# First stage of a hybrid decoder step: norm and scale in one VectorE instruction, the shift inside the rounding, scale and shift halves summed and turned separately

## The chip, the cores and the metric

The kernel runs on one core of one Trainium2 chip. The metric is device time in microseconds (us) of one execution, as the median of several runs. Engines are named TensorE (PE in the rows; PEld is its weight load), VectorE (DVE), ScalarE (ACT), GpSimd (POOL) and SyncE (SP, which issues most of the loads). Matmuls collect in PSUM; everything else lives in SBUF.

## The reference, cut to what matters

One inference step of a one-layer decoder on 512 prompt tokens and 8 sample tokens, width 1024. The first stage computes

```
mod = silu(c) @ w_mod + b_mod                 # shift, scale, gate, ... ; one row for the prompt, eight for the samples
h   = rmsnorm(x, norm1_g) * (1 + scale1) + shift1
u   = h @ w_in                                # first three column tiles of 128: f, q and output gate of head 0
```

The recurrences, the gates, the output projection and the MLP follow and are not touched by the change.

## The kernel before, in words

The tokens stand in the free dimension: activations are held turned, as 8 blocks k = 0..7 of 128 features by 520 tokens (512 of the prompt, 8 samples). Each matmul operand is split in a high half, rounded to the fast matmul format (`h_hi`, `whi`), and a low half, what the rounding lost (`h_lo`, `wlo`). A product (j, k) is six matmuls: weight tile j, block k, as high x high, high x low, low x high, for two halves of the tokens.

The first stage is written in `begin`. `load_x` asks for x; `norm_x` squares it on ScalarE and takes the root on VectorE with thirteen tiny operations (`rsqrt_small`); `transposed` turns all eight blocks of x on TensorE and copies them out of PSUM into `self.x`, half on ScalarE and half on VectorE; `normed` turns the roots into a row that lies on every partition (`rsb`). `scaled` multiplies a block by `rsb` into `u`. A **session** (k, part) is the product of silu(c) with 256 columns of `w_mod`, for blocks k and k + 1; part 1 is the scale, part 0 the shift. Both parts of a block pair go into the two halves of one PSUM tile. One ScalarE copy (`modev`) brings them out, and **turn** (`mod_close`) turns the four 128x128 squares and lets VectorE sum them and add the bias, into `modT`. Then `affine_split` makes the halves of two blocks: ScalarE computes the high half with scale and shift as it rounds, VectorE computes the same in full (`ht`) and subtracts. `high(j)` on ScalarE and `low(j)` on VectorE split weight tile j the same way; the third weight tile, `third` (tile `w` in the rows), is loaded last of the three.

The order on each engine is that of the code: `order("p", ...)`, `order("a", ...)` and `order("v", ...)` tie every instruction of TensorE, ScalarE and VectorE behind the one before it in program text. An engine works its queue strictly in that order, so an instruction that waits holds all behind it. SyncE's loads go out in the order in which `begin` asks for them. GpSimd issues the small parameter loads.

The three products j = 0, 1, 2 of the eight blocks are mixed with the sessions, so that TensorE has work while the next pair's scale and shift are made. `products((0, 2), ...)` are the first that need block pair 2, 3. In ScalarE's queue the high halves of that pair stand behind `high(2)`.

## Time and profile before

| what | value |
|---|---|
| median of 3 runs | 1004.61 us (1003.96 to 1005.44) |
| the profiled execution | 1004.8 us, its span from first to last instruction 1003.0 us |
| TensorE busy | 981.2 us, 98% of the span |
| VectorE, ScalarE, GpSimd busy | 694.2, 513.4, 112.4 us |
| TensorE idle until its first matmul | 3.11 us |

The first stage fills about the first 50 us. A busy share is a mean over all stages; what an edit is worth there is read from the waits of that stage. Line numbers Lnnn are those of the kernel before. In the rows "mm<-h,whi 128x260 x4" is four matmuls into tile `mm` from the tiles `h` and `whi`; what stands in brackets behind a row is how long the engine sat idle before it, and what ended that.

### The profile page before, as it was taken

How to read it: one execution, taken by the hardware profiler on the slowest of the kernel's cores; microseconds unless marked ns; L12 is line 12 of the kernel's file. 1: busy time of each engine (PE TensorE's matmuls, PEld its weight loads, DVE VectorE, ACT ScalarE, POOL GpSimd, SP SyncE). 2: the span in 40 equal slices, each digit the busy share in tenths (PEclk: the TensorE clock that was granted, in tenths of full speed). 3: DMA queues.
4: the chain of work that ended last, by engine and by line, in shares of the span. 5: the costliest groups of instructions: out<-in, count | busy, mean ns of one | idle time of the engine just before them, and what ended most of it. 6: DMA issues, size and time to landing. Idle time of an engine off the chain costs nothing.

```text
span 1003.0 us, 23261 instructions
## 1 busy us (share of the span) xinstructions
PE 981.2 (98%) x9585; PEld 954.5 (95%) x9585; DVE 694.2 (69%) x1546; ACT 513.4 (51%) x987; POOL 112.4 (11%) x194
## 2 busy tenths in 40 slices
PE   6999999999999999999999999999999999999996
PEld 4799999999999999999989999999999999999996
DVE  6789698697878867563332347767766776777686
ACT  5444844664584456351222234466556645646664
POOL 3000000000000000120000000012321331232151
PEclk9999999999999999999999999999999999999998
DMA  9885435344434434686567765222762483274242
GB/s 299 239 257 146 133 102 155 95 146 137 117 105 133 127 98 126 208 272 193 167 190 228 231 183 157 85 85 53 168 160 71 102 194 99 54 174 91 63 85 86
DMA packets 212572, 145.78 MB, mean 145 GB/s; under 512 B 6262, under 2 KB 196878, under 8 KB 212458
## 3 DMA queue, kind: packets, MB, share of 16 engines
q1 hardware_dynamic: 202562, 132.37, 44.5%
q0 software_dynamic: 9904, 11.92, 6.4%
q8 instruction: 75, 1.23, 0.5%
q14 instruction: 31, 0.25, 0.1%
HBM read 123.61 MB, written 13.39 MB: 137 GB/s over the span
## 4 chain that ended last, share of the span: by engine, by line
PE 93%; ACT 2%; SPq 2%; DVE 1%; DMA 1%; issue 1%; DVEq 0%; ACTq 0%
PE mm L120 67%; PE ps L1152 8%; PE pt L1152 4%; PE pb L1152 2%; PE ps L629 2%; PE ps L385 1%; PE pb L780 1%; DMA w<-in_w_in_dram 1%; SPq L374 1%; PE pt L705 1%; SPq L74 1%; PE pt L718 1%; PE pt L629 1%; PE pt L720 1%; PE ps L395 0%
## 5 line engine op out<-in xcount | busy, mean ns | idle before, releaser
L120 PE MATMUL mm<-h,whi 128*128 128x260 f32 x3040 | 502.8, 285 | 2.9 <-ACT h L481 1.9
L120 PEld LDWEIGHTS mm<-h,whi 128*128 128x128 f32 x3040 | 421.5, 189 | 8.4 <-ACT h L481 2.6
L120 PE MATMUL mm<-h,wlo 128*128 128x260 f32 x1520 | 310.8, 284 | 0.0
L85 ACT CAST whi<-wst 128x1024 fp32r<-128x1024 f32 x165 | 172.6, 1048 | 217.6 <-PE mm L120 178.7
L88 DVE TENSOR_TENSOR wlo<-wst,whi 128x1024 fp32r<-128x1024 f32 x165 | 201.2, 1220 | 89.6 <-ACT whi L85 88.2
L120 PEld LDWEIGHTS mm<-h,wlo 128*128 128x128 f32 x1520 | 237.0, 189 | 0.0
L120 PE MATMUL mm<-a,whi 128*128 128x260 f32 x512 | 82.8, 283 | 0.0
L120 PEld LDWEIGHTS mm<-a,whi 128*128 128x128 f32 x512 | 70.3, 188 | 0.9 <-issue 0.8
L120 PE MATMUL mm<-a,wlo 128*128 128x260 f32 x256 | 51.7, 284 | 0.0
L881 POOL DMA_DIRECT2D t<-oaT_d x8 | 4.3, 549 | 383.9 <-DMA oaT_d<-e 377.1
L1248 DVE TENSOR_TENSOR f<-f 128x260 f32<-128x260 f32 x64 | 27.3, 427 | 28.9 <-ACT f L1243 28.2
L1240 POOL TENSOR_TENSOR ft<-ft,fsh 128x8 f32<-128x8 f32 x28 | 18.4, 658 | 215.8 <-DVE ft L1234 215.8
L1237 ACT ACTIVATE ft<-ft,fsh 128x512 f32<-128x512 f32 (+2 forms) x36 | 24.1, 676 | 36.0 <-DVE ft L1234 36.0
L120 PE MATMUL mm<-b,whi 128*128 128x260 f32 x256 | 41.6, 284 | 0.0
L120 PEld LDWEIGHTS mm<-a,wlo 128*128 128x128 f32 x256 | 39.4, 188 | 0.0
L120 PEld LDWEIGHTS mm<-b,whi 128*128 128x128 f32 x256 | 35.0, 188 | 2.5 <-issue 2.5
L615 DVE TENSOR_TENSOR Y<-Y,tb 128x512 f32<-128x512 f32 x40 | 27.5, 687 | 9.1 <-PE ps L629 6.0
L1285 POOL DMA_DIRECT2D ma<-snap x28 | 26.8, 959 | 40.0 <-issue 22.1
L897 DVE TENSOR_TENSOR t<-mm,t 128x520 f32<-128x520 f32 x8 | 5.6, 699 | 37.0 <-PE mm L120 37.0
L1264 POOL DMA_DIRECT2D ma<-snap x28 | 26.6, 948 | 38.2 <-DMA ma<-snap 22.5
L1243 ACT ACTIVATE f<-ft 128x520 f32<-128x520 f32 (+1 forms) x36 | 20.7, 586 | 14.9 <-POOL ft L1241 12.9
L120 PE MATMUL mm<-b,wlo 128*128 128x260 f32 x128 | 25.8, 283 | 0.0
(489 smaller groups left out, 1839.2 us busy)
## 6 DMA issues: line engine op xcount, KB each, us to landing
wst<-in_w_in_dram SPq DMA_DIRECT2D x63, 512.0 KB
wm<-in_w_mod_dram SPq DMA_DIRECT2D x8, 2048.0 KB
wst<-in_w_ff_dram SPq DMA_DIRECT2D x32, 512.0 KB
wst<-in_w_ff_dram SPq DMA_DIRECT2D x64, 256.0 KB
wm<-in_w_mod_dram SPq DMA_DIRECT2D x8, 1024.0 KB
st<-in_state_hgrn_dram SPq DMA_DIRECT2D x8, 512.0 KB
vb<-vd SPq DMA_DIRECT2D x8, 512.0 KB
out_dram<-st SPq DMA_DIRECT2D x8, 512.0 KB
```

The costliest lines, as they stand in the source:

```text
L85: ins = self.nc.scalar.copy(hi, st)
L88: ins = self.nc.vector.tensor_tensor(lo, st, hi.bitcast(F32), OP.subtract)
L120: self.last_product = self.nc.tensor.matmul(out[:, :c.stop - c.start], x, y[:, c], start=first and n == 0, stop=last and n == 2)
L615: made = nc.vector.tensor_tensor(view(Y, b, 0, 2 * b, n, b), view(X, b, 0, 2 * b, n, b), fac, OP.mult)
L629: ins = nc.tensor.matmul(*args, start=True, stop=True)
L1152: ins = self.nc.tensor.matmul(ps, x[:, w], y[:, f], start=j in (1, 7, 2) and k == 0 and n == 0, stop=k == 3 and n == 2, skip_group_check=True)
L1237: nc.scalar.activation(t[:, :p], t[:, :p], AF.Relu, bias=sh[:, 0:1])
L1240: eng.tensor_tensor(t[:, p:], t[:, p:], sh[:, 1:9], OP.add)
L1243: nc.scalar.activation(f, self.two(self.ft)[:, a:a + n], AF.Square)
L1248: self.nc.vector.tensor_tensor(f[:, n], f[:, a], f[:, b], op)
L1264: nc.gpsimd.dma_start(x[1][:, b], v[:, :n], accum_op=OP.add)
L1285: nc.gpsimd.dma_start(x[t][:, a], s[p], accum_op=OP.add)
```

## The change

Norm and scale are applied in one VectorE instruction (`scaled`: x times scale times `rsb`, on the blocks of `self.x`, without `u`). The shift is added by ScalarE while it rounds (`hi`), and again in VectorE's subtraction (`lo`), which is now one instruction of three operands; the 8 sample columns have a small subtraction of their own. Each session has its own copy (`modev`, 256 wide) and its own turn of two squares; a pair's scale is applied ahead of its shift's session or beside it. The root's operations now stand in VectorE's order without copies between them. Only blocks 0 to 3 of x are turned at the start; 4 and 5 are turned behind the turn of the first shift, 6 and 7 behind product (1, 1), and all four are copied by ScalarE. The sample columns are copied to `self.x` by GpSimd. Weight tile 1 is asked for ahead of the scale part of pair 2. The space for descriptors of GpSimd's DMAs is set to 8192.

```diff
-    nc = bacc.Bacc("TRN2", target_bir_lowering=False, num_devices=1)
+    nc = bacc.Bacc("TRN2", target_bir_lowering=False, num_devices=1, dynamic_dma_scratch_size=SCRATCH)
...
+    def transposed_samples(self, order):
...
+        order("v", nc.vector.tensor_copy(xs, ps[:, :KO * NB].rearrange("p (k b) -> p k b", b=NB)))
         for k in range(KO):
-            nc.vector.tensor_copy(self.x[k][:, L:], ps[:, k * NB:(k + 1) * NB])
+            nc.gpsimd.tensor_copy(self.x[k][:, L:], xs[:, k])
...
+    def turned_x(self, outs, ts, order):
+        for t in ts:
+            for k, p in outs:
+                order("p", self.nc.tensor.transpose(p[:, t * 128:(t + 1) * 128], self.xn[:, t, k * 128:(k + 1) * 128], self.ident))
+
+    def copied_x(self, engine, k, p, order):
+        order(engine, (self.nc.scalar.copy if engine == "a" else self.nc.vector.tensor_copy)(self.x[k][:, :L], p))
...
+        order("v", nc.vector.tensor_tensor(xs, xs, p2[:, None, :NB].to_broadcast([128, KO, NB]), OP.mult))
...
-    def affine_split(self, k0, order):
...
-        hi = lambda j: order("a", nc.scalar.activation(self.h_hi[:, k0 + j, :L], u[:, k0 + j, :L], AF.Identity,
-                                                       bias=sh[:, j, 0:1], scale=sc[:, j, 0:1]))
-        full = lambda j: order("v", nc.vector.tensor_scalar(f[:, j, :L], u[:, k0 + j, :L], sc[:, j, 0:1], sh[:, j, 0:1], OP.mult, OP.add))
-        lo = lambda j: order("v", nc.vector.tensor_tensor(self.h_lo[:, k0 + j, :T], f[:, j], self.h_hi[:, k0 + j, :T].bitcast(F32), OP.subtract))
...
+    def scaled(self, k0, xs, order):
...
+            order("v", nc.vector.scalar_tensor_tensor(f[:, j, :L], self.x[k0 + j][:, :L], sc[:, j, 0:1], self.rsb, OP.mult, OP.mult))
...
+    def shifted(self, k0, f, order, between=None):
...
+            order("a", nc.scalar.activation(self.h_hi[:, k0 + j, :L], f[:, j, :L], AF.Identity, bias=sh[:, j, 0:1]))
...
+            order("v", nc.vector.scalar_tensor_tensor(self.h_lo[:, k0 + j, :L], f[:, j, :L], sh[:, j, 0:1],
+                                                      self.h_hi[:, k0 + j, :L].bitcast(F32), OP.add, OP.subtract))
...
+            ev = self.sm.tile([128, 256], F32, name="modev", bufs=2)
+            order("a", nc.scalar.copy(ev, ps))
+            return ev
+
+        def turn(k, part, ev):
...
+            for j in range(2):
+                order("p", nc.tensor.transpose(pt[:, j * 128:(j + 1) * 128], ev[:, j * 128:(j + 1) * 128], self.ident))
...
-        staged = [self._load_w(cols[0])]
+        staged = [self._load_w(cols[0]), self._load_w(cols[1])]
         load_mod(1, 2)
-        staged.append(self._load_w(cols[1]))
         load_mod(0, 2)
...
+        f = self.scaled(0, xs, order)
+        ev = session(0, 0)
         high(0)
-        low(0)
-        scaled(0, 1)
-        session(0, 1)
-        session(0, 0)
-        turn()
-        session(2, 1)
-        self.affine_split(0, order)
+        turn(0, 0, ev)
+        two = single()
+        self.turned_x(list(zip((4, 5), two)), range(NC), order)
+        self.shifted(0, f, order, lambda: low(0))
...
         products((0, 0), (0, 1))
-        session(2, 0)
+        ev = session(2, 1)
         products((1, 0))
+        turn(2, 1, ev)
+        f = self.scaled(2, xs, order)
+        products((1, 1))
+        two = single()
+        self.turned_x(list(zip((6, 7), two)), range(NC), order)
+        for k, p in zip((6, 7), two):
+            self.copied_x("a", k, p, order)
         exps, bounds_end = self.bounds(bounds, order)
-        turn()
-        products((1, 1))
+        ev = session(2, 0)
+        turn(2, 0, ev)
         high(2)
-        self.affine_split(2, order)
+        self.shifted(2, f, order)
```

On TensorE, from the turning of the roots (`pb`) to the first product, the kernel before has this (`mm` from `xn` are blocks 4 to 7 of x, `wm` the sessions, `modev` the turn):

```order
L467 MATMUL pb_304<-ident_111,rs16_y_220 128x128 x4
L458 MATMUL mm_282<-ident_111,xn_160 128x128 x4
L458 MATMUL mm_293<-ident_111,xn_160 128x128 x4
L469 MATMUL ps_309<-ident_111,rs16_y_220 128x8
L304 MATMUL ps_315<-ident_111,ra_157 128x16
L305 MATMUL ps_315<-ident_111,rm_153 128x64
L1617 MATMUL ps_338<-wm_183,cT_176 32x256 x8
L1617 MATMUL ps_338<-wm_185,cT_176 32x256 x8
L395 MATMUL ps_357<-ident_111,modev_355 128x128 x4
L1617 MATMUL ps_366<-wm_189,cT_176 32x256 x8
L120 MATMUL mm_332<-h_151,whi0_205 128x260 x2
```

After the change the same place reads (two of the eight turnings of blocks 4 and 5 into `pb` and `pt` shown):

```order
L472 MATMUL pb_293<-ident_111,rs16_y_265 128x128 x4
L474 MATMUL ps_298<-ident_111,rs16_y_265 128x8
L1628 MATMUL ps_313<-wm_183,cT_176 32x256 x8
L1639 MATMUL ps_324<-ident_111,modev_322 128x128 x2
L1628 MATMUL ps_313<-wm_185,cT_176 32x256 x8
L1639 MATMUL ps_324<-ident_111,modev_342 128x128 x2
L458 MATMUL pb_349<-ident_111,xn_160 128x128
L458 MATMUL pt_350<-ident_111,xn_160 128x128
```

The turnings of x have moved from beside the roots to behind the second session, each session is followed by a turn of its own, and the scale session of pair 2 (`wm_189`) is no longer ahead of the first product.

On ScalarE, ahead of the high halves (`h`) of pair 2, 3, the kernel before has:

```order
L1645 CAST whi1_207<-wst_191 128x1024
L1620 COPY modev_409<-ps_366 128x512
L1645 CAST whi2_209<-w3_195 128x1024
L481 ACTIVATE h_151<-xn_160,modT_182 128x512
L488 CAST h_151<-ht_442 128x2x8
```

After the change:

```order
L1666 CAST whi1_207<-wst_189 128x1024
L461 COPY ma_223<-pb_349 128x512
L461 COPY ma_224<-pt_350 128x512
L1630 COPY modev_394<-ps_385 128x256
L461 COPY ma_225<-pb_418 128x512
L461 COPY ma_226<-pt_419 128x512
L1630 COPY modev_447<-ps_385 128x256
L1666 CAST whi2_209<-w3_195 128x1024
L495 ACTIVATE h_151<-ht_408,modT_182 128x512
```

Four copies of x blocks (`ma`) and a second session copy now stand between the casts of weight tiles 1 and 2.

## Rows read from the trace of the kernel before

**Rows 1.** Stretches: PE, PEld, DVE, ACT, POOL busy (instructions), granted clock, DMA share, GB/s.

```profile
12.20:18.00 5.80, 5.78 (x26) 5.24 (x27) 2.83 (x13) 2.21 (x4) 0.00 (x0) 1.00 1.12 321
20.00:31.00 11.00, 8.57 (x92) 5.46 (x84) 9.71 (x26) 4.63 (x8) 0.00 (x0) 1.00 1.13 329
50.00:1003.00 953.00, 943.05 (x9269) 925.55 (x9267) 658.53 (x1423) 488.12 (x945) 103.75 (x171) 1.00 0.49 139
```

**Rows 2.** Chain of waits that ended last, 0 to 130 us: start, length, what.

```profile
19.20 10.89 DMA w<-in_w_in_dram
30.11 1.05 ACT whi L1645
31.16 0.72 ACT h L481
```

**Rows 3.** Timeline of TensorE: start us, us, what, idle time before it and releaser.

```profile
16.80 1.80 PE L458 MATMUL mm<-ident,xn 128*128 128x128 f32 x8
...
19.53 1.93 PE L1617 MATMUL ps<-wm,cT 128*32 128x256 f32 x32 [0.50 <-DVE c L472]
...
22.76 1.07 PE L1617 MATMUL ps<-wm,cT 128*32 128x256 f32 x16
...
27.54 1.07 PE L1617 MATMUL ps<-wm,cT 128*32 128x256 f32 x16
...
29.38 0.66 PE L395 MATMUL ps<-ident,modev 128*128 128x128 f32 x4
...
31.93 0.51 PE L120 MATMUL mm<-h,whi 128*128 128x260 f32 x2 [1.18 <-ACT h L481]
32.76 0.51 PE L120 MATMUL mm<-h,whi 128*128 128x260 f32 x2 [0.32 <-DVE h L484]
...
48.42 0.64 PE L120 MATMUL mm<-h,whi 128*128 128x260 f32 x4
...
49.14 0.94 PE L120 MATMUL mm<-h,whi 128*128 128x260 f32 x4
```

**Rows 4.** Timeline of VectorE, 11 to 20 us.

```profile
11.73 0.17 DVE L441 TENSOR_SCALAR ss<-ss 128x8 f32<-128x8 f32 x1 [3.03 <-ACT ht L439]
...
13.44 0.69 DVE L459 COPY ma<-mm 128x512 f32<-128x512 f32 x1
...
15.29 0.17 DVE L200 SCALAR_TENSOR_TENSOR rs_y<-rs_t,rs_y 128x8 f32<-128x8 f32 x1
17.97 1.43 DVE L459 COPY ma<-mm 128x512 f32<-128x512 f32 x2 [2.52 <-PE mm L458]
...
19.72 0.24 DVE L311 TENSOR_SCALAR pm<-pm 128x8 f32<-128x8 f32 x2
```

**Rows 5.** Timeline of ScalarE, 11 to 18 us.

```profile
11.60 1.05 ACT L459 COPY ma<-mm 128x512 f32<-128x512 f32 x2
...
17.05 0.59 ACT L471 COPY c<-pb 128x512 f32<-128x512 f32 x1 [0.27 <-PE pb L467]
```

**Rows 6.** TensorE's weight loads by line and shape, 0 to 50 us: count | busy, mean ns.

```profile
L458 PEld LDWEIGHTS mm<-ident,xn 128*128 128x128 f32 x32 | 5.9, 219 | 6.7 <-DMA xn<-in_x_prompt_dram 4.8 <-ACT ma L459 1.4 <-DVE ma L459 0.4
L395 PEld LDWEIGHTS ps<-ident,modev 128*128 128x128 f32 x16 | 1.7, 140 | 1.3 <-ACT modev L1620 1.2
```

**Rows 7.** Timeline of GpSimd: its last DMA issue of the first stage.

```profile
10.05 0.52 POOL L874 DMA_DIRECT2D out_dram<-in_state_conv_dram  x1
```

**Rows 8.** GpSimd's operations by line and shape, whole span.

```profile
L1240 POOL TENSOR_TENSOR ft<-ft,fsh 128x8 f32<-128x8 f32 x28 | 18.4, 658 | 215.8 <-DVE ft L1234 215.8
```

**Rows 9.** VectorE's operations by line and shape, 0 to 50 us and 53 to 110 us.

```profile
L1656 DVE TENSOR_TENSOR xn<-ma,c 128x520 f32<-128x520 f32 x8 | 5.1, 692 | 0.0
L483 DVE TENSOR_SCALAR ht<-xn,modT 128x512 f32<-128x512 f32 x8 | 4.3, 541 | 0.0
L1646 DVE TENSOR_TENSOR wlo<-wst,whi 128x1024 fp32r<-128x1024 f32 x2 | 2.4, 1221 | 0.1
...
L797 DVE SCALAR_TENSOR_TENSOR xc<-xb,pa,xc 128x509 f32<-128x509 f32 x2 | 1.5, 740 | 0.0
```

## Prediction

> **What bounds the kernel now.** I read the stretches of the span first [rows 1]. From 50 us on TensorE is busy for 943.05 of 953 us, so whatever the first stage gains or loses arrives at the end one for one; between 20 and 31 us it is busy for only 8.57 of 11. The change touches nothing behind the first stage: there each engine's instructions stand in the same order before and after. So the question is when the first stage's last products are done.

> Next the chain of waits [rows 2]. It comes down the load queue: the third weight tile (`third`, tile `w`) is issued at 19.20, and the cast of it on ScalarE starts at 30.11, when it has landed. That cast stands in ScalarE's queue ahead of the high halves of blocks 2 and 3, the next link at 31.16. TensorE's timeline says the same [rows 3]: done with product (1,1) at 30.75 it sits idle for 1.18 us and goes on at 31.93 with product (0,2), released by the high half; 0.32 us more go before 32.76 for its low half. I call 31.93 **the gate**. Behind it TensorE works almost without a hole: one small one is hidden in the row at 49.14, where four matmuls take 0.94 us and the like four at 48.42 take 0.64. A whole product, six matmuls, takes the 0.72 us between these two rows. What lies behind the gate is the same set of sessions, turns and products in both kernels. So the change can only pay by an earlier gate or by those holes, 0.32 and 0.3 us.

> **The load side of the gate.** The one edit in the load order moves the second weight tile ahead of a modulation tile. In front of `third` stand the same transfers with the same bytes, and the loads run without a pause (329 GB/s, DMA share 1.13 [rows 1]), so I leave its landing at 30.1. The modulation tile that is moved back, (1,2), was used at 22.76 [rows 3]; half a megabyte at 329 GB/s lies ahead of it now, 1.6 us, so it lands by 24.4. It will be wanted at 25.7 (below): hidden, with 1.3 us to spare.

> **The compute side, step by step** (times from the span's start).

> 1. Roots. Thirteen tiny VectorE operations begin at 11.73; two PSUM copies (one at 13.44) cut into them, and the last ends at 15.29 + 0.17 = 15.46 [rows 4]. The change puts the copies behind them. At their pace of 0.2 us they end at 14.1. Four transposes (half of the 1.80 that eight take at 16.80 [rows 3]), and the copy of `rsb`, 0.59 [rows 5]: ready at about 15.7, before at 17.05 + 0.59 = 17.64.
> 2. VectorE behind the roots: two copies, 1.43 for two, then the small parameter work, 17.97 + 1.43 = 19.40 to 19.96, 0.56 [rows 4]. That gives 16.1; one more multiplication (`xs`) 16.3.
> 3. Scale session of block pair 0. Its PSUM buffer comes free with the parameter copies, about 15.9. Two sessions take 1.93 at 19.53 [rows 3], so 1.0 each at that speed.
> 4. TensorE's speed. Loading a 128x128 operand of the same kind takes 219 ns in the x transposes, which run up to 18.5, and 140 ns in the modulation turns from 22.2 on [rows 6]. [...] (The granted clock of both stretches is printed as 1.00 [rows 1], so here only the durations show it.) After the change the block 4 to 7 transposes are gone from 12 to 18 us, and what is left there has holes: idle from about 12 (x is in when ScalarE's first copy of it starts at 11.60 [rows 5]) to 14.1, and waits for ScalarE behind each session. I take the low level for the first two sessions, the first turns and the first half of the transposes of blocks 4 and 5, and the high one from about 24 us, since from 21 to 24 us there is hardly a hole. A session at the low level: no row has one; between 1.0 (unchanged) and 2.0 (doubled); I take 1.0 x 219/140 = 1.55.
> 5. So: scale session 15.9 to 17.5; its copy is half as wide as the one that took 0.59 [rows 5], I take 0.4 between half and whole, plus 0.1 for the hand-over: 18.0; two transposes 0.5: 18.5; VectorE reduces, adds, multiplies, 0.6 at the pace of step 1, then two fused norm-and-scale instructions at 0.74 each, the price of the like instruction in [rows 9]: 20.6. Shift session 18.5 to 20.0, copied at 20.5, turned at 21.0, added at 21.4. The cast of the first weight tile now stands behind that copy: 20.5 to 21.5, so the high half of block 0 runs 21.5 to 22.3.
> 6. TensorE turns blocks 4 and 5 in 21.0 to 22.8 (1.80 for eight). The fused low half ends at 23.3, the low part of the first weight tile (1.22 [rows 9]) at 24.5, the low half of block 1 at 25.2; products (0,0) and (0,1) are done at 25.7. Before they were done at 27.5, when the next session starts [rows 3]. Up to here the change is **1.8 us ahead**.
> 7. From 25.7, fast: session (2,1) 1.0, product (1,0) 0.72, turn 0.3, product (1,1) 0.72, eight transposes of blocks 6 and 7 (four take 0.66 with the last one's tail [rows 3], so eight take 1.1), session (2,0) 1.0: 30.5. Before, eight of these transposes lay in front of 18.5 and session (2,1) beside other waits; here the lead is spent.
> 8. ScalarE has to copy blocks 6 and 7 first (two copies 1.05 [rows 5]): 29.6 to 30.6; then the session's copy 0.4: 31.0; only then the cast of the third weight tile, 31.0 to 32.0 in place of 30.11 to 31.16. VectorE's add is ready at 31.8. The high half starts at 31.95 in place of 31.1: **the gate moves by +0.85**, to 32.8, with its low half late by the same.
> 9. Behind the gate: two pairs of blocks whose turn is split in two, 0.1 for the extra switch on each: +0.2. The 0.3 in the row at 49.14 should go, as the low half there is one instruction: -0.3.

> Sum: 0.85 + 0.2 - 0.3 = **+0.75 us**. The profiled execution took 1004.8 (span 1003.0, 1.8 around it), so 1005.55 by its own time; the median of the runs shown is 1004.61, 0.2 lower: **1005.4 us**.

> **Edits that I cost at nothing.** VectorE does per block 0.69 (scaling by the root), 0.54 (scale and shift) and a subtraction of two SBUF tiles like the first before, now two fused instructions at 0.74 [rows 9]: over eight blocks some 3.5 us less, of which TensorE waits only at the low halves counted above. If that cover were gone, each would show at a low half. The smaller descriptor space for DMAs issued from GpSimd: GpSimd issues the same DMAs, and none of the first stage's steps waits for a late one. The eight sample copies go to GpSimd, behind its last DMA issue, which ends at 10.05 + 0.52 = 10.6 [rows 7]. VectorE's multiplication of `xs` must wait for them, and behind it stands the whole of block pair 0. No row has such a copy; the nearest small GpSimd operation takes 0.66 [rows 8]: all done by 15.9, before VectorE comes there at 16.1; a shorter one changes nothing. I take 0.
> [...]

> **The rivals.** *Low level until late (slower).* If TensorE is still at its low level when session (2,1) starts at 25.7, products (0,0) and (0,1), that session, product (1,0) and the turn pay together about 1.9 us more (0.4 for a product, 0.55 for the session, the rest by the same factor 1.56), all of it in front of the gate: +2.65, 1007.3; with the level rising only at 31, +3.6, 1008.2. The point that decides is whether it is up by 25.7. For it: TensorE idles where it worked through before, and behind each session it waits for ScalarE. Against it: from 21 to 24 it hardly waits. [...]
> *High level at once.* If it is up at 18.5 as before, the steps up to 30.1 come early enough that the landing of `third` alone sets the gate, as before: +0.2 - 0.3, 1004.5.
> *The lead is kept (faster).* If `third` lands 1.8 us earlier, at 28.3, and ScalarE's copies don't hold its cast back, the 1.8 us of step 6 survive: 1002.7. That needs 0.6 MB less ahead of it, against equal bytes in the queue.
> *GpSimd's copies are slow (slower).* From 0.7 us each they hold VectorE; at 1.5 they end at 22.6, block pair 0 is 6 us late, and after the slack of steps 6 to 8 some 4.4 us remain: 1009.0. Nothing in the rows is that slow.

> **How the numbers follow.** Main case 0.48, high level at once 0.14, low level until late 0.27 (0.22 of it above 2 us), lead kept 0.05, slow copies 0.06. Within 0.2%, 2 us, which is about what a measurement of this kernel can tell from no change, lie the first two and 0.05 of the third: 0.67; slower 0.22 + 0.06 = 0.28; faster 0.05. The range leaves out the lead, the slow copies and the latest clock: 1003.8 (the early case with 0.7 for the runs' own spread) to 1007.9. The main case alone spans 1004.6 to 1006.2, by a session at 1.0 or at 2.0.

> **What would show it.** Right: the roots end near 14.1; (0,1) is done near 25.7; the cast of the third weight tile starts late, near 31, with ScalarE busy ahead of it rather than waiting for the load; TensorE resumes near 32.8; the end moves by less than 1.5 us. Wrong: a cast at 30.1 with products at once (high level early, or the lead kept), operand loads of 219 ns beyond 26 us, or VectorE waiting for GpSimd at `xs`.

## The result: 0.3% slower, and the profile after

The changed kernel takes 1007.79 us, the median of seven runs (1006.07 to 1009.72), against 1004.58 for the kernel before (1003.96 to 1005.82, seven runs): a ratio of 1.003, interval 1.002 to 1.004. The range held it; the likeliest case, +0.75 us, was too small: the loss is 3.2 us. The profiled execution is the fastest of the seven, 1006.07 us with a span of 1004.3, only 1.3 us above the span before. So there are two losses to find: 1.3 us that this profile shows, and some 1.7 us, from it to the median, that it does not show.

TensorE's timeline answers [rows 3]. Columns as there.

```profile
15.55 1.93 PE L1628 MATMUL ps<-wm,cT 128*32 128x256 f32 x16
...
18.59 1.94 PE L1628 MATMUL ps<-wm,cT 128*32 128x256 f32 x16
...
21.50 0.42 PE L458 MATMUL pb<-ident,xn 128*128 128x128 f32 x1
...
22.96 0.27 PE L458 MATMUL pt<-ident,xn 128*128 128x128 f32 x1
23.00 0.51 PE L121 MATMUL mm<-h,whi 128*128 128x260 f32 x2
...
26.44 1.07 PE L1628 MATMUL ps<-wm,cT 128*32 128x256 f32 x16
...
30.17 1.07 PE L1628 MATMUL ps<-wm,cT 128*32 128x256 f32 x16
31.79 0.44 PE L1639 MATMUL ps<-ident,modev 128*128 128x128 f32 x2 [0.55 <-ACT modev L1630]
33.52 0.50 PE L121 MATMUL mm<-h,whi 128*128 128x260 f32 x2 [1.29 <-ACT h L495]
...
35.16 1.07 PE L1628 MATMUL ps<-wm,cT 128*32 128x256 f32 x16
...
38.74 1.07 PE L1628 MATMUL ps<-wm,cT 128*32 128x256 f32 x16
...
50.82 0.65 PE L121 MATMUL mm<-h,whi 128*128 128x260 f32 x4
```

The same session of sixteen matmuls takes 1.93 us at 15.55 and 1.07 at 26.44, and an x transpose 0.42 at 21.50 and 0.27 at 22.96: the low level until about 22.9, then the high one. (The granted clock is printed as 1.00 from the start to 50 us in this profile, so here again only the durations show the level.) The gate, 31.93 before, is at 33.52: +1.59. The hole before that row is as large as before (1.29, was 1.18); everything in front of it is late. The hole of 0.3 us in the row at 49.14 has no counterpart: the products of these microseconds take 0.65 for four matmuls, as at 50.82.

VectorE's timeline around the roots and ahead of the gate [rows 4]:

```profile
11.12 0.75 DVE L464 TENSOR_SCALAR ss<-ss 128x8 f32<-128x8 f32 x1 [2.72 <-ACT ht L438]
...
13.92 0.17 DVE L201 SCALAR_TENSOR_TENSOR rs_y<-rs_t,rs_y 128x8 f32<-128x8 f32 x1
...
15.68 0.21 DVE L477 TENSOR_TENSOR xs<-xs,ps 128x64 f32<-128x64 f32 x1
...
32.53 0.18 DVE L1644 TENSOR_TENSOR modT<-modT,pm 128x18 f32<-128x18 f32 x1
```

ScalarE's, the first high half and what stands ahead of the gate (the cast of [rows 2]):

```profile
22.23 0.72 ACT L495 ACTIVATE h<-ht,modT 128x512 fp32r<-128x512 f32 x1 [0.32 <-DVE modT L1644]
...
30.17 0.59 ACT L461 COPY ma<-pb 128x512 f32<-128x512 f32 x1 [2.17 <-PE pb L458]
30.65 0.59 ACT L461 COPY ma<-pt 128x512 f32<-128x512 f32 x1
31.36 0.37 ACT L1630 COPY modev<-ps 128x256 f32<-128x256 f32 x1
31.63 1.05 ACT L1666 CAST whi<-w 128x1024 fp32r<-128x1024 f32 x1
32.74 0.72 ACT L495 ACTIVATE h<-ht,modT 128x512 fp32r<-128x512 f32 x1
```

GpSimd's, the copies of the samples (behind the issue of [rows 7]) and what follows them:

```profile
10.09 1.06 POOL L451 COPY ma<-xs 128x8 f32<-128x8 f32 x8
...
11.32 0.52 POOL L1753 MEMSET at<- 128x512 f32 x1
```

In the kernel before, GpSimd's next work behind that issue is this:

```profile
37.65 0.29 POOL L1719 MEMSET fkq<- 128x96 f32 x2 [27.08 <-DVE xn L1656]
```

The roots end at 14.09, `xs` starts at 15.68 without a wait for GpSimd, and the third weight's cast waits for no load: it stands behind the two x copies and the session's copy. At the gate two chains end together: the cast at 31.63 + 1.05 = 32.68, the shift's add on VectorE at 32.53 + 0.18 = 32.71. The profile alone can't say which of them holds the high half at 32.74.

One row is out of place: the first operation on the roots takes 0.75 us, 0.17 before [rows 4]. It ends at 11.87, 0.03 us behind GpSimd's memset of `at`. The memsets of `fkq` and `at` serve a later stage. In the kernel before they wait until VectorE has made the last blocks of `u` (`xn`); the change has no `u`, and they follow the sample copies at once. In the profile of fill (below), a kernel with the change too, the same operation takes 0.99 us. That VectorE waits for GpSimd there is read from the two ends, 11.84 and 11.87, not tested. If it does, the change makes the roots about 0.6 us later than they could be, and TensorE is idle for 2.62 us until they are ready. No run moved the memsets, so what they cost at the end is not shown.

### The profile page after: what moved, and what is told of

Read it like the earlier page. It is cut to its first block, busy times and chain, and to the rows that moved or that the text cites. A ratio compares the mean times of both kernels' runs of the same rounds, so it can differ in the third digit from the quotient of the medians.

```text
span 1004.3 us, 23264 instructions
## 1 busy us (share of the span) xinstructions
PE 982.5 (98%) x9585; PEld 954.4 (95%) x9585; DVE 691.4 (69%) x1537; ACT 514.5 (51%) x993; POOL 113.3 (11%) x202
## 4 chain that ended last, share of the span: by engine, by line
PE 94%; DVE 2%; ACT 2%; DMA 1%; issue 1%; SPq 0%; ACTq 0%; DVEq 0%
PE mm L121 67%; PE ps L1162 8%; PE pt L1162 4%; PE pb L1162 2%; PE ps L639 2%; PE ps L386 1%; PE pb L790 1%; PE ps L1628 1%; PE pt L715 1%; PE pt L728 1%; DMA xn<-in_x_prompt_dram 1%; PE pt L639 1%; PE pt L730 1%; PE pt L747 0%; PE ps L396 0%
## 5 line engine op out<-in xcount | busy, mean ns | idle before, releaser
L625 DVE TENSOR_TENSOR Y<-Y,tb 128x512 f32<-128x512 f32 x40 | 27.5, 688 | 9.1 <-PE ps L639 6.0
L1295 POOL DMA_DIRECT2D ma<-snap x28 | 26.7, 966 | 39.2 <-issue 21.2
```

Source lines behind the costliest of these rows:

```text
L625: made = nc.vector.tensor_tensor(view(Y, b, 0, 2 * b, n, b), view(X, b, 0, 2 * b, n, b), fac, OP.mult)
L1295: nc.gpsimd.dma_start(x[t][:, a], s[p], accum_op=OP.add)
```

## Experiments

Two theories (the expectations of the first four runs call them queue theory and clock theory). **Chain**: the gate is late because the queue in front of it is (prediction steps 7 and 8), and the time follows the gate. **Level**: TensorE's clock costs, early in the stage and once more in the runs that the profile did not catch. The kernels that add transposes of the identity change no result; nobody reads what they write. The ratio is to the kernel before on the same chip, whose medians there were 1004.4 to 1005.1 us; it is not the quotient of the two medians.

| run | us, median (range, runs) | ratio (interval) |
|---|---|---|
| again | 1007.88 (1 run) | |
| after_late | 1008.28 (1 run) | |
| fill | 1007.09 (1005.51 to 1007.88, 11) | 1.0019 (1.001 to 1.0028) |
| early8 | 1006.47 (1005.53 to 1007.14, 11) | 1.0013 (1.0005 to 1.0022) |
| gatefill | 1006.24 (1005.35 to 1007.79, 11) | 1.0013 (1.0005 to 1.0022) |
| holes | 1004.61 (1004.0 to 1005.55, 11) | 0.9995 (0.9986 to 1.0004) |
| s20_early | 1005.69 (1004.43 to 1007.18, 11) | 1.0008 (0.9999 to 1.0017) |
| holes_early | 1006.91 (1005.19 to 1007.76, 11) | 1.002 (1.0011 to 1.0029) |
| joint | 1014.04 (1012.94 to 1014.68, 5) | 1.0087 (1.0075 to 1.0099) |
| before_fill | 1004.39 (1003.91 to 1008.3, 12) | 0.9997 (0.9988 to 1.0006) |
| s20_table | 1004.6 (1003.8 to 1005.73, 11) | 0.9993 (0.9984 to 1.0002) |
| best | 1004.57 (1003.38 to 1005.55, 11) | 0.9993 (0.9985 to 1.0002) |

**again**: the changed kernel once more, unedited, for a second profile.

> The changed kernel once more, for a second profile. Clock theory (TensorE stays at or falls back to its low level for a stretch that differs from run to run, because the change leaves holes in its work before 26 us): sessions, turns and products that take twice their time will stand in other places than in the first profile, and the end moves with their number, anywhere from +0.7 to +5 us against before. Queue theory (what costs is that each session waits for its own copy and turn, and that copies stand ahead of the third weight tile's cast; the clock is beside the point): the first product of block 2 starts at 33.5 again, and the span is +1.3 us again.

It took 1007.88 us, 1.8 more than the first profile, with the gate 0.17 us earlier, at 33.35. Its stretches around the gate (granted clock third from the end):

```profile
32.00:34.00 2.00, 0.56 (x3) 0.30 (x2) 1.16 (x5) 1.94 (x5) 0.00 (x0) 1.00 1.09 348
34.00:36.00 2.00, 1.68 (x16) 1.13 (x20) 2.00 (x3) 1.70 (x5) 0.00 (x0) 0.78 1.09 349
36.00:38.00 2.00, 2.00 (x16) 1.19 (x7) 0.06 (x1) 0.37 (x1) 0.00 (x0) 0.50 1.09 348
```

and its TensorE timeline there:

```profile
35.00 1.89 PE L1628 MATMUL ps<-wm,cT 128*32 128x256 f32 x16
36.81 1.24 PE L121 MATMUL mm<-h,whi 128*128 128x260 f32 x4
...
40.16 1.07 PE L1628 MATMUL ps<-wm,cT 128*32 128x256 f32 x16
```

**after_late**: is the cast in ScalarE's queue the gate (step 8)?

```
+        self.shifted(2, f, order)
         high(2)
-        self.shifted(2, f, order)
         low(2)
-        exps()
-        (table load)
...
         ev = session(4, 1)
+        exps()
+        (table load)
```

> The changed kernel with the cast and low part of the third weight tile, the two exponentials and the table load put behind the high halves of block pair 2 on ScalarE. If the cast in ScalarE's queue is the gate (step 8 of the forecast): the first product of block 2 starts 0.8 to 1.0 us earlier relative to the end of that pair's shift session. If the turn of the shift is the gate (VectorE's add ended 0.03 us before the high half in the profile after): no change in that distance, 2.3 us from the session's end to the high half.

TensorE's timeline from session (2,0) to the gate:

```profile
29.60 1.07 PE L1628 MATMUL ps<-wm,cT 128*32 128x256 f32 x16
...
32.95 0.52 PE L121 MATMUL mm<-h,whi 128*128 128x260 f32 x2 [1.29 <-ACT h L495]
33.92 0.80 PE L121 MATMUL mm<-h,whi 128*128 128x260 f32 x2 [0.45 <-DVE h L500]
...
40.97 1.07 PE L1628 MATMUL ps<-wm,cT 128*32 128x256 f32 x16
```

and ScalarE's high half:

```profile
32.17 0.72 ACT L495 ACTIVATE h<-ht,modT 128x512 fp32r<-128x512 f32 x1 [1.01 <-DVE modT L1644]
```

The cast is out of the way, and session (2,0) to gate is 32.95 - 29.60 = 3.35 us, in the first profile 33.52 - 30.17 = 3.35. ScalarE now waits for the shift's add alone. So the cast is not the gate; the row of session, copy, turn, reduction, add and high half is. The level falls again behind the gate (0.80 for two matmuls that took 0.51), and the time is 1008.28 in spite of a gate 0.57 earlier. This fall costs more: from the gate to session (4,0) it takes 40.97 - 32.95 = 8.02 us, in the first profile 38.74 - 33.52 = 5.22, so 2.80.

**fill and early8**: the high level earlier. One puts 12 idle transposes ahead of the turned roots and 2 behind each of the first two sessions, the other turns all eight x blocks at the start, with useful transposes.

```
+        fill(12)
         self.normed(roots, xs, order)
         ev = session(0, 1)
+        fill(2)
         turn(0, 1, ev)
```

> Twelve transposes of the identity into an unused PSUM tile ahead of the roots' turning, two behind each of the first two sessions; nothing reads them. Clock theory: TensorE is fast from about 16 us in every run, sessions take 1.0 us and not 1.9, the first product of block 2 starts at 32 to 32.6, and the runs lie within 2 us of each other, 0 to +0.8 us against before. Queue theory: no gain, +1.3 us in the profile and about +3 in the median as without the filling.

```
         self.turned_x([(k, mm[k // 2][:, k % 2]) for k in range(4)], range(NC), order)
         roots = self.roots(ss, order)
+        self.turned_x(list(zip((4, 5), two)), range(NC), order)
...
+        self.turned_x([(6, more[:, 0]), (7, more[:, 1])], range(NC), order)
```

> The changed kernel with all eight blocks of x turned and copied at the start again (blocks 4 and 5 into the two single PSUM tiles, 6 and 7 into a third double one, copies on ScalarE). Clock theory: dense work from 10 us on, so fast before 18 us; the landing of the third weight tile near 30 is the gate again as before the change, first product of block 2 at 31.5 to 32, end between -0.7 and +0.3 us. Queue theory, copies of x ahead of the cast: also gained, but only the 1.1 us of two copies and the 0.9 of eight transposes; sessions still at 1.9 where holes remain, end +0.5 or more.

TensorE's timeline of fill:

```profile
15.67 1.07 PE L1628 MATMUL ps<-wm,cT 128*32 128x256 f32 x16 [0.61 <-DVE pm L308]
...
21.14 0.51 PE L121 MATMUL mm<-h,whi 128*128 128x260 f32 x2 [0.67 <-ACT h L495]
...
23.24 0.51 PE L121 MATMUL mm<-h,wlo 128*128 128x260 f32 x2 [0.63 <-DVE wlo L1667]
...
25.07 1.94 PE L1628 MATMUL ps<-wm,cT 128*32 128x256 f32 x16
...
33.17 0.52 PE L121 MATMUL mm<-h,whi 128*128 128x260 f32 x2 [1.29 <-ACT h L495]
```

One stretch of early8 (granted clock third from the end):

```profile
23.00:29.00 6.00, 5.82 (x33) 4.32 (x34) 1.92 (x3) 0.37 (x1) 0.00 (x0) 0.50 1.12 327
```

Both get the first sessions at 1.07 us, and both lose the level again: with the early work done sooner, TensorE now waits ahead of the first high half too (0.67 us in fill, 1.54 in early8, not at all in the first profile), the level falls behind the holes of the first products, and the gate is where it was (33.17, 33.26). Neither came out as the clock theory had it (at most +0.8 and +0.3 us); what fill gains, 1.0019 against 1.003, lies within overlapping intervals, and its profile has a second fall behind the gate. Idle or useful, the transposes raised the level: in fill TensorE does nothing but transposes from 5.71 to 13.99, the twelve idle ones last (2.65 us), and the four that turn the roots behind them take 0.65 us, for 1.11 in the first profile.

**gatefill and holes**: ten idle transposes at the gate alone, and transposes in all holes that are free.

```
+        fill(acc[2][1], 10)
         products((0, 2))
         ev = session(4, 1)
```

> The changed kernel with ten idle transposes where TensorE waits for the high half of the third block (31.8 to 33.5 us in its profile); no engine waits for their result. Theory 'level': what lies beyond the later gate is a second fall of the clock, since the records of two of the four runs before show half speed from 34 or 35 us for 3.4 us, one from 33.3 us for 6.8 us, and the profile with none there is the fastest; then the gate stays at 33.3 to 33.6 us, no stretch after it stands at 0.50, and the median falls from 1007.8 to 1005.9 to 1006.4 us. Theory 'chain': the time is set by the session, its copy, its turn and the adds alone; the transposes do nothing useful, and the median stays at 1007.4 to 1008.0 us.

holes has this line, those of fill, and one more:

```
+        fill(acc[1][:, 0], 6)
         products((0, 0), (0, 1))
```

> Idle transposes in all holes: 12 before the roots are turned, 2 behind each of the first two sessions, 6 before the first products, 10 before the products of the third block. Theory 'level': the granted clock is 1.00 from 13.7 us on without a fall; sessions take 1.07 us each, the first products end at 24.9 us, the session (2,0) starts at 28.3 us and the gate comes 3.35 us behind it, at 31.7 us; the median is 1004.0 to 1004.8 us. Theory 'chain': with the same waits for ScalarE and VectorE the gate stays at 33.2 us and the median at 1006.5 to 1007.1 us, as in the run with the early transposes alone.

TensorE's timeline of gatefill:

```profile
32.23 1.26 PE L1651 MATMUL pt<-ident 128*128 128x128 f32 x10
33.69 0.50 PE L121 MATMUL mm<-h,whi 128*128 128x260 f32 x2 [0.20 <-ACT h L495]
```

That of holes:

```profile
18.21 1.07 PE L1628 MATMUL ps<-wm,cT 128*32 128x256 f32 x16
...
28.92 1.07 PE L1628 MATMUL ps<-wm,cT 128*32 128x256 f32 x16
...
32.27 0.50 PE L121 MATMUL mm<-h,whi 128*128 128x260 f32 x2 [0.20 <-ACT h L495]
```

Both came out as 'level' had it. gatefill leaves the gate late (33.69) and its profile has no fall behind it: 1006.24, where 'chain' wanted 1007.4 or more; three of its eleven runs are still at 1007.5 to 1007.8, and its interval overlaps that of the changed kernel a little (1.002 to 1.0022). Every run on record has the mean granted clock of its whole span, and this fits: in gatefill 0.997 or 0.998 for the eight runs up to 1006.64 us, 0.995 or 0.996 for the three slow ones; in the changed kernel 0.997 for the fastest run, 0.994 to 0.996 for the six others. A difference of 0.002 in 1004 us is 2 us. (The mean can't place a fall: it holds the end of the span too, where the granted clock stands at 0.50 for the last 5 us, in the profile before and in the one after.) With the level up from the second session on, holes has session (2,0) at 28.92, the gate 3.35 us behind it, and the loss is gone: ratio 0.9995, no change from the kernel before. Session and gate are 0.6 us later than expected; x comes later in this run, the last four transposes of it ahead of the roots start at 10.63 for 9.89 us. The useful work and its order are those of the changed kernel.

**s20_early and holes_early**: session (2,0) ahead of product (1,1), its turn ahead of the x transposes, whose copies go behind the high halves; without and with idle transposes.

```
+        ev = session(2, 0)
         products((1, 1))
+        turn(2, 0, ev)
         (x transposes of blocks 6 and 7)
-        (their copies)
-        ev = session(2, 0)
-        turn(2, 0, ev)
         high(2)
         self.shifted(2, f, order)
+        (their copies)
```

> The changed kernel with the session (2,0) ahead of products (1,1) and its turn ahead of the turning of x blocks 6 and 7, whose copies go behind the high halves. Theory 'chain': the session starts at 28.4 us, its turn ends at 30.5 us, VectorE's sums follow the two scale instructions (30.8 us) and end at 31.5 us, the gate is at 32.2 us instead of 33.5; the median falls by 1.3 us, to 1006.5 us. Theory 'level': the hole ahead of the gate shrinks from 1.3 us to some 0.6, the fall behind 34 us becomes rare, and the median is 1004.8 to 1005.5 us: both the gate and the second fall are gone.

> Both edits together: idle transposes in the holes, and the session (2,0) ahead of products (1,1). Both theories: clock 1.00 from 13.7 us on, session (2,0) at 26.7 us if its weights have landed, gate at 30.5 to 31.2 us (then the cast of the third weight on ScalarE may hold it, its load landed at 29 to 30 us). Theory 'level' gives 1003.2 to 1004.0 us, below the kernel before (1004.4); theory 'chain' 1005.0 to 1006.0 us, since it allots only the gate's 2.3 us.

TensorE's timeline of s20_early:

```profile
18.54 1.41 PE L1628 MATMUL ps<-wm,cT 128*32 128x256 f32 x16
...
25.63 1.07 PE L1628 MATMUL ps<-wm,cT 128*32 128x256 f32 x16
...
31.27 0.51 PE L121 MATMUL mm<-h,whi 128*128 128x260 f32 x2 [0.42 <-ACT h L495]
```

That of holes_early, behind its x transposes:

```profile
32.42 1.31 PE L1651 MATMUL pt<-ident 128*128 128x128 f32 x10 [2.10 <-ACT ma L461]
```

The gate moves by 2.25 us, to 31.27, ahead of the kernel before, and the idle time there from 1.29 to 0.42. Of this 0.81 us is not the edit: in this run the level rose within the second session (1.41 us), and session (2,1) starts at 25.63 for 26.44. From there to the gate it takes 5.64 for 7.08, so the edit moves it by 1.44, near the 1.3 of 'chain'. The ratio 1.0008 is no longer to be told from no change. Its runs go from 1004.43 to 1007.18: 'level' was too hopeful by 0.2, 'chain' too dear by 0.8. holes_early missed both theories, in its profile by my own edit: its idle transposes write to a PSUM tile that comes free with the x copies, now behind the high halves, and so waited 2.10 us and held the gate themselves. The profiled run is the fastest, 1005.19; the eight runs above 1006.8 have a mean granted clock of 0.994 to 0.996, the three others 0.997, which fits a fall behind this hole.

**joint**: the halves of a block copied, turned and added in one piece again, the scale instruction behind that.

```
-            ev = self.sm.tile([128, 256], F32, name="modev", bufs=2)
-            order("a", nc.scalar.copy(ev, ps))
-            return ev
+            if not part:
+                ev = self.sm.tile([128, 512], F32, name="modev", bufs=1)
+                order("a", nc.scalar.copy(ev, opened.pop(k)[0]))
...
-        f = self.scaled(0, xs, order)
         ev = session(0, 0)
         high(0)
         turn(0, 0, ev)
+        f = self.scaled(0, xs, order)
```

> The changed kernel with one of its parts undone: both halves of a block are again copied, turned and added in one piece behind the second session, and the scale instruction follows. Theory 'chain': VectorE's two scale instructions (1.41 us) now stand between the adds and the high half; with the 0.59 us copy in place of 0.37 and four turns for two, the first products come 1.4 to 1.9 us later (24.5 to 25 us), the gate at 36 to 36.8 us (33.5 in the changed kernel); 1010 to 1012 us. Theory 'the separate turns are what costs': with one copy and one turn as before, the gate returns to 32 to 33 us and the time to 1004.5 to 1006 us.

TensorE's timeline from the first product to the gate:

```profile
23.05 0.82 PE L121 MATMUL mm<-h,whi 128*128 128x260 f32 x2 [1.66 <-ACT h L495]
...
27.32 1.94 PE L1628 MATMUL ps<-wm,cT 128*32 128x256 f32 x16
...
31.74 1.07 PE L1628 MATMUL ps<-wm,cT 128*32 128x256 f32 x16
...
36.68 1.03 PE L121 MATMUL mm<-h,whi 128*128 128x260 f32 x2 [2.45 <-ACT h L495]
```

The gate is at 36.68, in the range of 'chain', but half of that is luck. From session (2,0) to the gate it takes 4.94 us for 3.35, which is 'chain'. The other half is not: the first product starts at 23.05, not at 24.5 to 25, and session (2,0) is 1.57 us late because the level was low in front of it (0.82 for the first two matmuls, 1.94 for session (2,1)). At the gate it is low again (1.03 for two matmuls that took 0.51), and the time lies above the 1012 of 'chain'. So the separate halves are not what costs. With the scale instruction between the two turns, they save the changed kernel some 6 us (1.0087 against 1.003), the falls that their lack brings included.

**before_fill, s20_table and best**: does the kernel before lose its slower runs with nine idle transposes at its gate? And does the changed one win with the session moved, the table load of ScalarE (1.28 us in the first profile) behind the copy of session (4,1), and (best) the idle transposes of the first stage?

```
+        fill(acc[2][1], 9)
         products((0, 2))
```

> The kernel before with nine idle transposes where its TensorE waits 1.18 us for the high half of the third block (30.75 to 31.93 us). Theory 'level': the slower runs of the kernel before (1005.2, and 1006 to 1007 us, beside many at 1004.0 to 1004.5) are the same fall of the clock after this hole; they go, and the median of its runs falls to 1004.0 to 1004.4 us with the highest under 1005.5. Theory 'chain': the spread has another cause and stays: median 1004.5 to 1005.1, highest 1006.5 to 1007 us.

```
         low(2)
-        exps()
-        (table load)
...
         ev = session(4, 1)
+        exps()
+        (table load)
```

> The changed kernel with the session (2,0) ahead of products (1,1), as in the run before, and the exponentials and the table load of ScalarE behind the copy of session (4,1), which waited for them (TensorE then idled 0.55 us at 35 us). No idle transposes. Theory 'level': gate at 31.3 us; the idle 0.55 us and one chance of a fall are gone; median 1004.4 to 1005.2 us (1005.7 without the second move), with some runs at 1006 us where the clock still falls. Theory 'chain': 0.5 us less than before the second move, 1005.2 us, with the same spread of 2.7 us.

best has this, the moves of s20_early, and the idle transposes of holes but those at the gate.

> Both moves of the run beside it, and the idle transposes in the first stage only (12 ahead of the turned roots, 2 behind each of the first two sessions, 6 ahead of the first products), none at the gate, where the run with both edits made them wait for copies of ScalarE. Theory 'level': clock 1.00 from some 14 us on without a fall, session (2,0) at 27.2 us, gate at 30.7 us; median 1003.0 to 1003.8 us, below the kernel before, with a spread under 1.5 us. Theory 'chain': the gate's 0.6 us less than in the run beside it, and the same spread: 1004.3 to 1004.8 us.

TensorE's timeline of before_fill:

```profile
27.52 1.94 PE L1617 MATMUL ps<-wm,cT 128*32 128x256 f32 x16 [0.37 <-DMA wm<-in_w_mod_dram]
```

That of s20_table:

```profile
26.79 1.90 PE L1628 MATMUL ps<-wm,cT 128*32 128x256 f32 x16
...
33.26 0.51 PE L121 MATMUL mm<-h,whi 128*128 128x260 f32 x2 [0.42 <-ACT h L495]
```

That of best:

```profile
24.70 1.94 PE L1628 MATMUL ps<-wm,cT 128*32 128x256 f32 x16
...
31.66 0.51 PE L121 MATMUL mm<-h,whi 128*128 128x260 f32 x2 [0.42 <-ACT h L495]
```

before_fill has the median of 'level', 1004.39, but not its end to the slower runs: they reach 1008.3, and in its profile session (2,0) takes 1.94 us, so the fall there comes earlier than the gate, behind the holes of the first products. Its four slowest runs have a mean granted clock of 0.995 or 0.996, the eight others 0.997 or 0.998. s20_table has the median of 'level', but its one profile, of its slowest run (1005.73), has not the gate: the level falls at 25 us, and the gate is at 33.26, not 31.3. The level of best, too, falls at 24 us: the gate is at 31.66, not 30.7, and the median 0.8 us above the top of 'level', in the range of 'chain'; it has the lowest run of all, 1003.38. Neither is shown to be faster than the kernel before.

## Why the prediction was right in range and too low in its likeliest case

- **That the range held is luck in part.** 1007.79 lies 0.1 us under its top, the prediction gave 0.67 to a time within 2 us of no change, and half of the loss is in none of its terms.
- **Steps 1, 2, 3: right in time, the first by luck.** Roots at 14.09 (14.1), `rsb` at 15.88 (15.7), `xs` at 15.68 (16.1), first session at 15.55 (15.9). The roots could start 0.6 us sooner than in the profile before (11.12 for 11.73) and lost as much beside GpSimd's memsets, a cost that the prediction has nowhere.
- **The sample copies, taken at 0.** GpSimd's eight copies take 1.06 us together and don't hold `xs`, so the rival of slow copies falls. But they and the memsets that now follow them overlap the start of the roots, where the first operation takes 0.75 for 0.17.
- **Step 4: the right level, mis-sized.** The low level was taken for the first two sessions and did hold there, but a session costs 1.93 at it, not 1.55, for 1.07 at the high one: the time nearly doubles, and the ratio 219/140 of operand loads was the wrong measure. Two sessions in a row make it 0.76. With these the sum gives 1005.55 + 0.76 = 1006.3 for the profiled execution, which took 1006.07. The level rose at 22.9, which is before 25.7, the point that was to decide. No row of before shows the 2.0 that step 4 sets as an upper bound; sessions wholly at the low level take 1.93 or 1.94 in the runs. That holes in TensorE's work keep the level low was the author's estimate; in fill, with the early holes filled, the first session took 1.07.
- **Steps 5 to 7: late by that, otherwise right.** The first session starts 0.35 early, and the two turns at the low level give that back (0.69 each for 0.5). The high half of block 0 runs from 22.23 (21.5), released by the shift's add and not by the cast, (0,1) is done at 26.5 (25.7), and from there to the end of session (2,0) it takes 4.8 us, as worked out.
- **Step 8: the gate late by the same 0.7, with the wrong cause.** 33.52 for 32.8. The cast behind ScalarE's copies ends beside the add, but after_late took it away and the 3.35 us stayed.
- **Step 9: right in sign.** From the gate (+1.59) to the end (+1.3) 0.3 us come back (0.1 forecast). The 0.1 for each split turn was an estimate that no run shows apart.
- **What no step had.** "Behind it TensorE works almost without a hole" looked at holes behind the gate and not at what the hole before it can do: the level that had risen falls again. One fall is 1.58 us by rows (2.80 in after_late); 1006.07 + 1.58 = 1007.65, near the median of 1007.79. Both profiles that keep the early stage and this hole as they were, again and after_late, have it, and gatefill takes most of it off. The mean granted clocks fit it too. That the seven runs differ by just this is still argued; only one of them has a profile, and the two at 1009.5 and 1009.7 lie above what a fall of 1.58 or 2.80 us gives.
- **Rivals.** "Low level until late" came near in number (1007.3) but not in place: the level was up at 25.7. "High level at once" was tried in holes and holds in number: no loss (its 1004.5 against 1004.61). Its path does not: the gate is at 32.27, 3.35 us behind session (2,0), and not set by the landing of the third weight tile. "The lead is kept" didn't happen.

Open: why a hole of one length brings a fall in one run and none in the next; what the memsets on GpSimd cost at the end; and what sends some runs of the kernel before to 1006 and 1007 us. Of the fourteen such runs on record beside the experiments, eleven have a mean granted clock of 0.993 to 0.996, but three have 0.997 or 0.998, so the clock can't be all of it.

## What to carry to other kernels

When work is taken off an engine or put in another order, ask what TensorE's idle time does to its clock: here the loss of 3 us went when TensorE was kept busy and the changed instructions were left as they were (holes), and most of it when one session was put earlier (s20_early). Price the low level by nearly doubling a whole row (1.94 for 1.07), and look behind TensorE's holes for a fall, not only for a late rise. Look also at what a change sets free on engines that it hardly touches: memsets of a later stage came to stand beside the roots. Where a profile is faster than the median, take a second one before explaining the difference.

## What the runs showed that was not expected

- Once risen, the level fell again in the first stage in eight of fourteen profiles, between 22 and 37 us, at the holes of the first products or that of the gate; in the six others it stayed up, with holes of the same length among them. Of the five profiles with a hole of 1.29 us at the gate, three have a fall behind it (again, after_late, fill) and two have none (the profile after, early8).
- Transposes of 128x128 alone, twelve in a row, raised the level: in fill the next session took 1.07 us for 1.93.
- Raising the level earlier (fill) brought the next hole earlier and a fall with it: of what it gained, no more than 0.35 us arrived at the gate.
- The first operation on the roots, 0.17 us on VectorE before, took 0.75 us in the profile after and ended there 0.03 us behind GpSimd's last memset; in that of fill it took 0.99 us.
